# Output projection with the branch gate folded into w_out, a one-operation residual, and a separate pool for the head tiles

## The chip, the cores and the metric

The kernel runs as one program on one core of a Trainium2 chip. The metric is device time in microseconds (us) of one execution. All tensors are float32; large products are made of three float32r matmuls of a high and a low part (hi*hi, hi*lo, lo*hi).

## The reference, cut to what matters

One trunk layer over 2048 latent tokens of width 1024, with 256 context tokens as a prefix:

```
sh1, sc1, g1, sh2, sc2, g2 = split(silu(c) @ ada_w + ada_b, 6)
y = concat([rg_out, hg_out]) @ w_out        # RG-LRU heads and HGRN2 heads, both directions
h = layer_norm(ALPHA * h + g1 * y, ln1_g, ln1_b)
u2 = h * (1 + sc2) + sh2
f = hier_moe(u2)                            # top group, top 2 of its 8 experts, SwiGLU
h = layer_norm(ALPHA * h + g2 * f, ln2_g, ln2_b)
```

The gate g1 is a row of 1024 numbers, one for each output column of w_out.

## The kernel before

The kernel has four stages. A start of some 50 us makes the modulation of x. The **projection** (`project`, lines 773 to 870) runs to about 1049 us: 156 slots, each one projection of one 128-column unit of `w_in` over one block of tokens, in three passes over the tokens. After each slot the string `TURNS` says in which order evacuation, a step of the HGRN2 scan (`Head.run`), a step of the RG-LRU (`Lru`) and a filler step are issued. The **output stage** (lines 888 to 1212), here called stage F, takes the 16 tiles of 128 tokens through the output projection, the first layer norm and the router. Then come the expert blocks and the second layer norm.

What matters here in the projection: `mods` (line 362) is a generator that computes the rest of the modulation rows on GpSimd (POOL). Each of its 8 groups of 512 columns makes 8 loads of `ada_w` into the tile `mraw`, a multiplication (L371 or L373) and an addition (L374) on POOL for each, and a store to the DRAM row `modD` (L382); that is 17 steps a group, one or two steps a slot where no other filler waits. Groups 0 and 1 are g1. In the last pass the head scans store their backward states `kb` to `sbD` from POOL's queue (L556), and the RG-LRU stores its result `hb` to `rgD` the same way (L645). In the last six slots `wo_fetch` (L761) loads the 8 row blocks of `w_out` on SyncE (SP), and `wo_split` divides each into `woh` (a copy on ScalarE, ACT, L244) and `wol` (a subtraction, L245, on VectorE, DVE, but block 1 on POOL: `SPOOL = (1,)`). Block j = 7 is loaded into the buffer that block 1 had, so its load waits for block 1's split. The pools `hgp` (the heads' tiles), `tmp` and `ca` are closed together after the projection (`big.close()`), and all tiles of stage F are then laid in their place.

In stage F the order on every engine is written out by the loop of line 1155. In turn j it issues, among others: `post` of the previous tile's second half, `stats1`, the first `outproj` half of tile j (24 matmuls of 512 columns, with 8 transposes of a finished tile among them), `norm1`, part of the router's `top2`, `affine`, the rest of `top2` (L1079, L1081, L1083), `post` of tile j's first half, the multiplication L963 and the split L966/L972 (`mh` on ACT, `ml` on DVE) of the next tile's input, the second `outproj` half with the router's matmuls, and `place`. For the 10 tiles below token 1280 `head_norm` adds 4 small matmuls and `head_sum` a DVE addition (L942). `post` is:

```
dve.tensor_mul(r[:, s], d["ps"], g1[:, s])                                  # L991: PSUM times SBUF
dve.scalar_tensor_tensor(r[:, s], d["x"][:, s], ALPHA, r[:, s], ...)        # L992: SBUF and SBUF
dve.bn_stats(d["bs"][:, nh, :], r[:, s])                                    # L993
```

`affine` makes u2 on DVE (L1009, L1010) and at the same time scales the residual row on POOL (L1011, L1012, two operations over 128x1024 in SBUF). `constants` (L902) loads five rows broadcast to 128 partitions, 512 KB each (g1, l1g, l1b, l2g, l2b), and the router's weights; `loads` (L914) fetches a tile's inputs three turns ahead, all on SP.

Of the kernel before, what the change touches and what calls it, by code (L numbers as in the profile page):

```python
# [19 lines left out]
D = 1024  # L20
# [18 lines left out]
LE = L + 128  # L39
NRAW, NUP, NDOWN = 8, 9, 4  # L40
NWR, NUR = 2, 4
SPOOL = (1,)
EXTRA = (-9, -8, -2, -1)
MODS = (4, 8, 4)

# [29 lines left out]
def hymba_kernel(ctx, tc, xT, ctxT, x, small, rows, ada_w, w_in, gate_w, w_out, router_w, w1, w3, w2, out):  # L75
# [2 lines left out]

    dram = ctx.enter_context(tc.tile_pool(name="dram", bufs=1, space=DRAM))
    modD = dram.tile([1, 4096], F32, name="modD")  # L80
    oD = dram.tile([L, 512], F32, name="oD")
    hgD = dram.tile([512, L], F32, name="hgD")
    rgD = dram.tile([512, L], F32, name="rgD")
# [11 lines left out]
    big = ctx.enter_context(ExitStack())  # L95
    upool = early.enter_context(tc.tile_pool(name="upool", bufs=1))
    fk = early.enter_context(tc.tile_pool(name="fk", bufs=1))
    hgp = big.enter_context(tc.tile_pool(name="hgp", bufs=1))
    tmp = big.enter_context(tc.tile_pool(name="tmp", bufs=2))
    ca = big.enter_context(tc.tile_pool(name="ca", bufs=1))  # L100
    ident = const.tile([128, 128], F32, name="ident")
    make_identity(nc, ident)
    sm = ca.tile([128, 108], F32, name="sm")
# [246 lines left out]
    def proj(w, u, n, between, mid=3):  # L350
# [38 lines left out]
    class Head:  # L389
# [46 lines left out]
        def run(self):  # L436
# [108 lines left out]
            if p == 2:  # L545
                cur = S[:, h, 0, :]
                for half in (1, 0):
                    kb = hgp.tile([128, 5, 128], F32, name="kb", tag=f"keep{1 - half}")
                    carry = tmp.tile([128, 128], F32, name="carry", tag="S00", bufs=1)
                    for c in range(4, -1, -1):  # L550
                        if c == 4:
                            dve.tensor_copy(kb[:, c, :], cur)
                        nxt = kb[:, c - 1, :] if c else carry
                        dve.scalar_tensor_tensor(nxt, kb[:, c, :], fbs[:, h, 5 * half + c:5 * half + c + 1], U1[half][:, c, :], op0=ALU.mult, op1=ALU.add)
                    cur = carry
                    pool.dma_start(sbD[h][:, 640 * half:640 * half + 640], kb.rearrange("p c v -> p (c v)"))  # L556
                    yield


# [194 lines left out]
    def wo_fetch(m):  # L754
        while len(wraw) < min(m, KC):
            j = len(wraw)
            if j in (4, 5):
                wraw.append(upool.tile([128, D], F32, name="wr", tag="wr", bufs=2))
            else:
                wraw.append(fk.tile([128, D], F32, name="wor", tag="FK"[j % 2], bufs=2))  # L760
            sp.dma_start(wraw[j], w_out[128 * j:128 * j + 128, :])  # L761

    def wo_split():
        for j in range(KC):
# [106 lines left out]

    project()
    start.close()
    big.close()

    def rows_to(pl, name, lo, n=D, src=None):
        t = pl.tile([128, n], F32, name=name)
# [8 lines left out]
        return r  # L886

    with ExitStack() as st:
        fc = st.enter_context(tc.tile_pool(name="fc", bufs=1))
        fp = st.enter_context(tc.tile_pool(name="fp", bufs=2))  # L890
        fs = st.enter_context(tc.tile_pool(name="fs", bufs=2))
        st.enter_context(tc.manual_schedule())
        fk4 = [fk.tile([128, 2 * W], F32, name=n, tag=t, bufs=2) for n, t in (("g1", "F"), ("l1g", "K"), ("l1b", "F"), ("l2g", "K"))]
        g1, l1g, l1b, l2g = (t[:, :D] for t in fk4)
        l2b = fc.tile([128, D], F32, name="l2b")
        sc2 = fp.tile([128, D], F32, name="fu")
        rw = fk4[3][:, D:D + 40 * KC].rearrange("p (k e) -> p k e", e=40)
        rb = fc.tile([128, 40], F32, name="rb")
        dve.memset(rb[:, 4:8], FAR)
        dve.memset(rw[:, :, 4:8], 0.0)  # L900

        def constants():  # L902
            for t, src, lo in ((g1, modD, 0), (l1g, rows, 4096), (l1b, rows, 4096 + D), (l2g, modD, 2 * D), (l2b, modD, D), (rb[:, 0:4], rows, 4096 + 4 * D), (rb[:, 8:40], rows, 4100 + 4 * D)):
                n = t.shape[-1]
                sp.dma_start(t, src[0:1, lo:lo + n].to_broadcast([128, n]))
            rk = router_w.rearrange("(k p) e -> p k e", p=128)
# [7 lines left out]
        def loads(i):  # L914
            r0 = 128 * i
            d = M[i] = {}
            d["o"] = fp.tile([128, 4, 128], F32, name="fo", bufs=3)
            sp.dma_start(d["o"].rearrange("p h v -> p (h v)"), oD[r0:r0 + 128, :])
            if i < SPILL // 128:
                d["qb"] = fp.tile([128, 4, 128], F32, name="fqb", bufs=3)  # L920
                sp.dma_start(d["qb"], qbD[:, :, r0:r0 + 128].rearrange("h p t -> p h t"))
                d["sb"] = fp.tile([128, 4, 128], F32, name="fsb", bufs=3)
                sp.dma_start(d["sb"], sbD[:, :, r0:r0 + 128].rearrange("h p v -> p h v"))
            d["hg"] = fp.tile([128, 4, 128], F32, name="fhg", bufs=3)
            sp.dma_start(d["hg"], hgD[:, r0:r0 + 128].rearrange("(h p) t -> p h t", p=128))
            d["m"] = fp.tile([128, KC, 128], F32, name="fm", bufs=3)
            sp.dma_start(d["m"][:, 0:4, :], rgD[:, r0:r0 + 128].rearrange("(h p) t -> p h t", p=128))
            d["x"] = fp.tile([128, D], F32, name="fx", bufs=4)
            sp.dma_start(d["x"], x[r0:r0 + 128, :])
# [58 lines left out]
        def post(i, nh):  # L988
            d = M[i]
            r, s = d["r"], slice(512 * nh, 512 * nh + 512)  # L990
            dve.tensor_mul(r[:, s], d["ps"], g1[:, s])  # L991
            dve.scalar_tensor_tensor(r[:, s], d["x"][:, s], ALPHA, r[:, s], op0=ALU.mult, op1=ALU.add)  # L992
            dve.bn_stats(d["bs"][:, nh, :], r[:, s])  # L993

        def stats1(i):
# [4 lines left out]

        def norm1(i):
            r, mv, rs = (M[i][k] for k in ("r", "mv", "rs"))
            dve.scalar_tensor_tensor(mv[:, 0:1], mv[:, 0:1], -1.0, rs, op0=ALU.mult, op1=ALU.mult)
            act.activation(r, r, AF.Identity, scale=rs, bias=mv[:, 0:1])

        def affine(i):
# [29 lines left out]
        def top2(i):  # L1036
# [30 lines left out]
            yield  # L1067
            dve.max_index(ei, em, el)

            dve.tensor_sub(c[:, 3:4], em[:, 1:2], em[:, 0:1])  # L1070
            act.activation(c[:, 4:5], c[:, 3:4], AF.Exp)
            dve.tensor_copy(ee, ei[:, 0:2])
            yield
# [6 lines left out]
            yield  # L1080
            dve.reciprocal(wt[:, 0:1], c[:, 5:6])  # L1081
            yield
            dve.tensor_mul(wt[:, 1:2], wt[:, 0:1], c[:, 4:5])  # L1083

        def count(i):
            ee, ho, both = E.pop(i)
# [624 lines left out]
```

## Time and profile before

| what | value |
|---|---|
| median of 3 runs | 2267.64 us (2263.36 to 2269.0) |
| the profiled execution, its own time | 2266.98 us |
| its span from first to last instruction | 2265.3 us |
| TensorE matmul (PE) busy | 2055.4 us, 91% of the span |
| VectorE (DVE) busy | 1756.6 us, 78% |
| ScalarE (ACT) busy | 1167.5 us, 52% |
| GpSimd (POOL) busy | 667.9 us, 29% |
| mean granted TensorE clock | 0.956 of full speed |

Shares are averages over stages with different limits. In a timeline a row gives the start in us, the duration in us, engine, line, operation, output <- input, shape, count, and in brackets the idle time of that engine before it with what ended it. "x2" is two instructions merged. A duration holds also the time in which an instruction that has been started waits for a port.

### The profile page before, as it was taken

How to read it: one execution, taken by the hardware profiler on the slowest of the kernel's cores; microseconds unless marked ns; L12 is line 12 of the kernel's file. 1: busy time of each engine (PE TensorE's matmuls, PEld its weight loads, DVE VectorE, ACT ScalarE, POOL GpSimd, SP SyncE). 2: the span in 40 equal slices, each digit the busy share in tenths (PEclk: the TensorE clock that was granted, in tenths of full speed). 3: DMA queues.
4: the chain of work that ended last, by engine and by line, in shares of the span. 5: the costliest groups of instructions: out<-in, count | busy, mean ns of one | idle time of the engine just before them, and what ended most of it. 6: DMA issues, size and time to landing. Idle time of an engine off the chain costs nothing.

```text
span 2265.3 us, 34490 instructions
## 1 busy us (share of the span) xinstructions
PE 2055.4 (91%) x12440; PEld 1812.5 (80%) x12440; DVE 1756.6 (78%) x2665; ACT 1167.5 (52%) x1863; POOL 667.9 (29%) x507
## 2 busy tenths in 40 slices
PE   7999999999999999996899986999999999999970
PEld 3888788999988989986777775888888888888850
DVE  6677776766776898897788885788887778787869
ACT  3456554644654554654333323556666556566633
POOL 5122233223233130001555552122222222222216
PEclk9999999999999999998999996999999999999985
DMA  8233243323324143228555316789999898999965
GB/s 265 105 103 116 80 137 115 109 81 119 117 97 136 57 161 142 70 105 289 181 163 168 131 56 250 220 291 291 302 312 303 287 300 294 292 300 314 330 223 238
DMA packets 176275, 433.16 MB, mean 191 GB/s; under 512 B 26837, under 2 KB 68821, under 8 KB 175590
## 3 DMA queue, kind: packets, MB, share of 16 engines
q1 hardware_dynamic: 151846, 378.36, 47.7%
q0 software_dynamic: 14448, 45.23, 8.2%
q10 hardware_dynamic: 9808, 7.34, 1.0%
q8 instruction: 99, 1.62, 0.3%
q14 instruction: 74, 0.61, 0.1%
HBM read 354.43 MB, written 76.43 MB: 190 GB/s over the span
## 4 chain that ended last, share of the span: by engine, by line
PE 54%; DVE 20%; DMA 10%; ACT 6%; issue 6%; POOL 2%; SPq 1%; POOLq 0%; DVEq 0%; ACTq 0%
PE pp L354 8%; PE pp L355 8%; PE pp L356 8%; PE ph L1434 5%; PE pa L472 4%; DMA X<-u2D,ix 3%; DVE wlo L1297 3%; PE pg L596 3%; PE ph L1435 2%; PE pye L1324 2%; DMA ix<-idxD 2%; PE pye L1325 2%; PE pye L1323 2%; DVE fr L992 2%; PE ph L1379 2%
## 5 line engine op out<-in xcount | busy, mean ns | idle before, releaser
L1297 DVE TENSOR_TENSOR wlo<-raw,whi 128x1024 fp32r<-128x1024 f32 x384 | 452.3, 1221 | 56.4 <-ACT whi L1296 52.9
L354 PE MATMUL pp<-uh,wh 128*128 128x384 f32 (+2 forms) x1248 | 444.9, 356 | 3.2 <-ACT wh L244 1.8
L355 PE MATMUL pp<-ul,wh 128*128 128x384 f32 (+2 forms) x1248 | 428.8, 344 | 5.3 <-DVE ul L245 4.9
L356 PE MATMUL pp<-uh,wl 128*128 128x384 f32 (+2 forms) x1248 | 427.2, 342 | 3.2 <-DVE wl L245 3.2
L1296 ACT CAST whi<-raw 128x1024 fp32r<-128x1024 f32 x384 | 382.4, 1050 | 39.3 <-PE pye L1324 23.0
L1434 PE MATMUL ph<-xw,whi 128*128 128x448 f32 (+3 forms) x896 | 257.6, 363 | 1.6 <-DVE hid L1385 1.6
L354 PEld LDWEIGHTS pp<-uh,wh 128*128 128x128 f32 x1248 | 238.1, 191 | 23.7 <-ACT rgs L597 5.2
L355 PEld LDWEIGHTS pp<-ul,wh 128*128 128x128 f32 x1248 | 238.1, 191 | 20.8 <-DVE ul L245 11.2
L356 PEld LDWEIGHTS pp<-uh,wl 128*128 128x128 f32 x1248 | 237.4, 190 | 13.2 <-DVE wl L245 4.3
L1435 PE MATMUL ph<-xw,wlo 128*128 128x224 f32 (+3 forms) x896 | 221.7, 247 | 0.0
L373 POOL TENSOR_SCALAR mraw<-mraw,sil 128x512 f32<-128x512 f32 x56 | 103.1, 1842 | 358.3 <-DMA mraw<-in_ada_w_dram 358.3
L1333 POOL DMA_INDIRECT accD<-y,ix x46 | 107.7, 2341 | 315.0 <-DVE y L1332 302.3
L1377 PE MATMUL ph<-whi,xx 128*80 128x256 f32 (+3 forms) x608 | 176.0, 290 | 4.7 <-DMA raw<-in_w_dram 3.6
L1434 PEld LDWEIGHTS ph<-xw,whi 128*128 128x128 f32 x896 | 173.3, 193 | 7.2 <-DVE hid L1385 1.8
L1435 PEld LDWEIGHTS ph<-xw,wlo 128*128 128x128 f32 x896 | 176.0, 196 | 1.2
L1379 PE MATMUL ph<-wlo,xx 128*80 128x256 f32 (+3 forms) x608 | 173.1, 285 | 1.9 <-DVE wlo L1297 1.9
L1378 PE MATMUL ph<-whi,xx 128*80 128x256 f32 (+3 forms) x608 | 172.0, 283 | 0.0
L1306 POOL DMA_INDIRECT X<-u2D,ix x46 | 70.1, 1525 | 322.2 <-DMA ix<-idxD 202.8
L472 PE MATMUL pa<-Q,km 128*128 128x128 f32 x896 | 125.5, 290 | 16.1 <-DVE Q L475 10.3
L472 PEld LDWEIGHTS pa<-Q,km 128*128 128x128 f32 x896 | 120.3, 196 | 21.3 <-ACT km L462 7.1
L245 DVE TENSOR_TENSOR wl<-wr,wh 128x1024 fp32r<-128x1024 f32 x84 | 107.9, 1285 | 37.2 <-ACT wh L244 37.1
L982 PE MATMUL py<-woh,mh 128*128 128x512 f32 x256 | 116.6, 455 | 16.3 <-ACT mh L966 16.3
(351 smaller groups left out, 4552.3 us busy)
## 6 DMA issues: line engine op xcount, KB each, us to landing
raw<-in_w_dram SPq DMA_DIRECT2D x384, 512.0 KB
wr<-in_w_in_dram SPq DMA_DIRECT2D x84, 512.0 KB
mraw<-in_ada_w_dram SPq DMA_DIRECT2D x64, 256.0 KB
aw<-in_ada_w_dram SPq DMA_DIRECT2D x16, 512.0 KB
fx<-in_x_dram SPq DMA_DIRECT2D x16, 512.0 KB
accD<-fr SPq DMA_DIRECT2D x16, 512.0 KB
u2D<-fu SPq DMA_DIRECT2D x16, 512.0 KB
f<-accD SPq DMA_DIRECT2D x16, 512.0 KB
```

The source lines that it names most:

```text
L354: pe.matmul(ps, wh[:, k, :], uh[:, k, :], start=k == 0, stop=False)
L355: pe.matmul(ps, wh[:, k, :], ul[:, k, :], start=False, stop=False)
L356: pe.matmul(ps, wl[:, k, :], uh[:, k, :], start=False, stop=k == KC - 1)
L472: pe.matmul(pa[:, c, :], km[:, s:s + 128], cut(Q, s, [(2 * b, 64 // b), (T + b, 2), (1, b)]), start=True, stop=True)
L982: pe.matmul(ps, mh[:, k, :], wo[k][0][:, s], start=k == 0, stop=False)
L1296: act.copy(hi, raw)
L1297: dve.tensor_sub(lo, raw, hi.bitcast(F32))
L1377: pe.matmul(p, self.xh[:, k, :], wh[:, kk, :], start=k + g == 0, stop=False, skip_group_check=True)
L1378: pe.matmul(p, self.xl[:, k, :], wh[:, kk, :], start=False, stop=False, skip_group_check=True)
L1379: pe.matmul(p, self.xh[:, k, :], wl[:, kk, :], start=False, stop=k == KC - 1, skip_group_check=True)
L1434: pe.matmul(p[:, :2 * n], wh[:, kk, f], self.x[:, k].rearrange("p h t -> p (h t)"), start=k == 0, stop=False)
L1435: pe.matmul(p[:, :n], wl[:, kk, f], self.x[:, k, 0, :], start=False, stop=k == KC - 1)
```

## The change

w_out is multiplied by the gate once, column by column, while the projection runs: a new generator `gated`, called by `mods` after groups 0 and 1, broadcasts 512 gate values to 128 partitions, and for each of 8 row blocks loads 128x512 of `w_out`, multiplies on POOL and stores to a DRAM tensor `woD` from POOL's queue. `wo_fetch` reads `woD`. `post` is then one operation on PSUM and x, and the load of g1 in `constants` goes. The heads' pool `hgp` lies on the other side of the memory and is closed first; a pool `fl` with the loaded inputs of stage F takes its place. All splits of w_out are on DVE, the `sbD` stores go from POOL's queue to SP's, two memsets from DVE to POOL, and four tiny operations of two tensors become operations of a tensor and a per-partition scalar.

```diff
-SPOOL = (1,)
+SPOOL = ()
...
+    woD = dram.tile([D, D], F32, name="woD")
...
-    hgp = big.enter_context(tc.tile_pool(name="hgp", bufs=1))
     tmp = big.enter_context(tc.tile_pool(name="tmp", bufs=2))
     ca = big.enter_context(tc.tile_pool(name="ca", bufs=1))
+    heads = ctx.enter_context(ExitStack())
+    hgp = heads.enter_context(tc.tile_pool(name="hgp", bufs=1, side="right"))
...
+    def gated(nh):
+        s = slice(512 * nh, 512 * nh + 512)
+        g = tmp.tile([128, 512], F32, name="g1h", tag="macc", bufs=1)
+        sp.dma_start(g, modD[0:1, s].to_broadcast([128, 512]))
+        for k in range(KC):
+            raw = tmp.tile([128, 512], F32, name="wog", tag="mraw", bufs=1)
+            sp.dma_start(raw, w_out[128 * k:128 * k + 128, s])
+            yield
+            pool.tensor_mul(raw, raw, g)
+            pool.dma_start(woD[128 * k:128 * k + 128, s], raw)
+            yield
...
             sp.dma_start(modD[:, 512 * g:512 * g + 512], r)
+            if g < 2:
+                yield from gated(g)
...
-                    pool.dma_start(sbD[h][:, 640 * half:640 * half + 640], kb.rearrange("p c v -> p (c v)"))
+                    sp.dma_start(sbD[h][:, 640 * half:640 * half + 640], kb.rearrange("p c v -> p (c v)"))
...
-            sp.dma_start(wraw[j], w_out[128 * j:128 * j + 128, :])
+            sp.dma_start(wraw[j], woD[128 * j:128 * j + 128, :])
...
     project()
     start.close()
-    big.close()
+    heads.close()
...
+        fl = st.enter_context(tc.tile_pool(name="fl", bufs=3, side="right"))
+        big.close()
...
-        dve.memset(rb[:, 4:8], FAR)
-        dve.memset(rw[:, :, 4:8], 0.0)
 
         def constants():
-            for t, src, lo in ((g1, modD, 0), (l1g, rows, 4096), ...
+            pool.memset(rb[:, 4:8], FAR)
+            pool.memset(rw[:, :, 4:8], 0.0)
+            for t, src, lo in ((l1g, rows, 4096), ...
...
-            d["o"] = fp.tile([128, 4, 128], F32, name="fo", bufs=3)
+            d["o"] = fl.tile([128, 4, 128], F32, name="fo", bufs=3)
...
-            dve.tensor_mul(r[:, s], d["ps"], g1[:, s])
-            dve.scalar_tensor_tensor(r[:, s], d["x"][:, s], ALPHA, r[:, s], op0=ALU.mult, op1=ALU.add)
+            dve.scalar_tensor_tensor(r[:, s], d["x"][:, s], ALPHA, d["ps"], op0=ALU.mult, op1=ALU.add)
...
-            dve.scalar_tensor_tensor(mv[:, 0:1], mv[:, 0:1], -1.0, rs, op0=ALU.mult, op1=ALU.mult)
+            dve.tensor_scalar(mv[:, 0:1], mv[:, 0:1], rs, -1.0, op0=ALU.mult, op1=ALU.mult)
...
-            dve.tensor_sub(c[:, 3:4], em[:, 1:2], em[:, 0:1])
+            dve.tensor_scalar(c[:, 3:4], em[:, 1:2], em[:, 0:1], None, op0=ALU.subtract)
...
-            dve.tensor_mul(wt[:, 1:2], wt[:, 0:1], c[:, 4:5])
+            dve.tensor_scalar(wt[:, 1:2], wt[:, 0:1], c[:, 4:5], None, op0=ALU.mult)
```

## Rows read from the trace of the kernel before

**Rows 1.** Windows view, stage F: busy PE, PEld, DVE, ACT, POOL; clock, DMA.

```profile
1200.00:1250.00 50.00, 45.36 (x242) 38.17 (x241) 44.58 (x107) 19.24 (x57) 25.94 (x27) 0.97 0.56 174
```

**Rows 2.** Starts of post for tiles 3 and 16, from the chain of waits.

```profile
1107.90 0.70 DVE fr L991
...
1343.29 0.69 DVE fr L991
```

**Rows 3.** Timeline of TensorE from one tile's first matmul to the next.

```profile
1222.98 0.48 PE L982 MATMUL py<-woh,mh 128*128 128x512 f32 x1
1224.07 0.50 PE L983 MATMUL py<-woh,ml 128*128 128x512 f32 x1 [0.61 <-DVE ml L972]
...
1230.36 1.05 PE L936 MATMUL pob<-fsb,fqb 128*128 128x128 f32 x8
...
1240.82 0.49 PE L982 MATMUL py<-woh,mh 128*128 128x512 f32 x1 [1.23 <-ACT mh L966]
```

**Rows 4.** Timeline of VectorE in one turn of stage F.

```profile
1215.00 0.21 DVE L1079 TENSOR_SCALAR c<-c 128x1 f32<-128x1 f32 x1
...
1215.45 1.90 DVE L1083 TENSOR_TENSOR tok<-tok,c 128x1 f32<-128x1 f32 x1
1217.27 0.68 DVE L991 TENSOR_TENSOR fr<-py,g 128x512 f32<-128x512 f32 x1
1217.98 2.38 DVE L992 SCALAR_TENSOR_TENSOR fr<-fx,fr 128x512 f32<-128x512 f32 x1
```

**Rows 5.** Timeline of GpSimd in the same turn.

```profile
1213.91 3.43 POOL L1011 TENSOR_TENSOR fr<-fr,l1g 128x1024 f32<-128x1024 f32 x1 [2.83 <-DVE fu L1009]
1217.41 2.40 POOL L1012 TENSOR_TENSOR fr<-fr,l1b 128x1024 f32<-128x1024 f32 x1
```

**Rows 6.** All instructions of three lines: count, then shortest/median/longest in ns.

```profile
L992 DVE SCALAR_TENSOR_TENSOR fr<-fx,fr x32: 691/1139/2383, 1080.9 to 1348.6; 128x512 f32<-128x512 f32 x32
...
L1083 DVE TENSOR_TENSOR tok<-tok,c x16: 160/1900/1917, 1124.7 to 1372.2; 128x1 f32<-128x1 f32 x16
...
L1079 DVE TENSOR_SCALAR c<-c x16: 205/206/208, 1124.2 to 1371.7; 128x1 f32<-128x1 f32 x16
```

**Rows 7.** A wide tensor-with-scalar operation of the projection, all 48 of its line.

```profile
L404 DVE TENSOR_SCALAR F<-F,omlb,lbc x48: 399/476/1470, 53.1 to 953.2; 128x384 f32<-128x384 f32 x32, 128x256 f32<-128x256 f32 x8, 128x512 f32<-128x512 f32 x8
```

**Rows 8.** Timeline of VectorE from the projection's end into stage F.

```profile
1051.27 0.06 DVE L899 MEMSET rb<- 128x4 f32 x1 [1.68 <-DMA sbD<-kb]
...
1052.79 4.51 DVE L245 TENSOR_TENSOR wol<-wor,woh 128x1024 fp32r<-128x1024 f32 x2
...
1062.49 0.09 DVE L900 MEMSET l2g<- 128x32 f32 x1
...
1075.13 0.69 DVE L1181 TENSOR_SCALAR fu<-l2g 128x1024 f32<-128x1024 f32 x1 [3.69 <-DMA l2g<-modD]
```

**Rows 9.** Timelines of GpSimd, SyncE's queue and TensorE over the same stretch.

```profile
1065.13 0.20 POOL L884 TENSOR_SCALAR rstd<-ms 128x4 f32<-128x4 f32 x1 [8.91 <-ACT g L950]
...
1045.68 10.89 SPq L761 DMA_DIRECT2D wor<-in_w_out_dram  x2
...
1070.22 0.79 PE L982 MATMUL py<-woh,mh 128*128 128x512 f32 x1 [1.91 <-ACT mh L966]
```

**Rows 10.** Timeline of VectorE behind the last tile.

```profile
1358.68 2.24 DVE L1097 TENSOR_TENSOR ho<-ho,pos 128x64 f32<-128x64 f32 x1
```

**Rows 11.** Additions and stores of mods; SyncE's longest waits: total, times, longest us.

```profile
L374 POOL TENSOR_TENSOR macc<-macc,mraw x56: 1262/1294/2275, 83.3 to 841.9; 128x512 f32<-128x512 f32 x56
...
L382 SPq DMA_DIRECT2D modD<-mr x8: 231/242/251, 166.9 to 859.2; - x8
...
SPq L234 <- DVE wl L245: 508.3, 71, 20.1
SPq L368 <- POOL macc L374: 82.7, 18, 8.5
```

**Rows 12.** The eight stores of sbD from GpSimd's queue (tile view): time to landing.

```profile
DMA to landing us min/median/max: 7.7/7.8/7.9
```

More of the change, by code (lines that the diff above doesn't have):

```diff
@@ L892, in hymba_kernel @@
         st.enter_context(tc.manual_schedule())
-        fk4 = [fk.tile([128, 2 * W], F32, name=n, tag=t, bufs=2) for n, t in (("g1", "F"), ("l1g", "K"), ("l1b", "F"), ("l2g", "K"))]
-        g1, l1g, l1b, l2g = (t[:, :D] for t in fk4)
+        fk4 = [fk.tile([128, 2 * W], F32, name=n, tag=t, bufs=2) for n, t in (("sq", "F"), ("l1g", "K"), ("l1b", "F"), ("l2g", "K"))]
+        l1g, l1b, l2g = (t[:, :D] for t in fk4[1:])
         l2b = fc.tile([128, D], F32, name="l2b")
@@ L898, in hymba_kernel @@
         rb = fc.tile([128, 40], F32, name="rb")
-        dve.memset(rb[:, 4:8], FAR)
-        dve.memset(rw[:, :, 4:8], 0.0)
         def constants():
-            for t, src, lo in ((g1, modD, 0), (l1g, rows, 4096), (l1b, rows, 4096 + D), (l2g, modD, 2 * D), (l2b, modD, D), (rb[:, 0:4], rows, 4096 + 4 * D), (rb[:, 8:40], rows, 4100 + 4 * D)):
+            pool.memset(rb[:, 4:8], FAR)
+            pool.memset(rw[:, :, 4:8], 0.0)
+            for t, src, lo in ((l1g, rows, 4096), (l1b, rows, 4096 + D), (l2g, modD, 2 * D), (l2b, modD, D), (rb[:, 0:4], rows, 4096 + 4 * D), (rb[:, 8:40], rows, 4100 + 4 * D)):
                 n = t.shape[-1]
@@ L916, in loads @@
             d = M[i] = {}
-            d["o"] = fp.tile([128, 4, 128], F32, name="fo", bufs=3)
+            d["o"] = fl.tile([128, 4, 128], F32, name="fo", bufs=3)
             sp.dma_start(d["o"].rearrange("p h v -> p (h v)"), oD[r0:r0 + 128, :])
             if i < SPILL // 128:
-                d["qb"] = fp.tile([128, 4, 128], F32, name="fqb", bufs=3)
+                d["qb"] = fl.tile([128, 4, 128], F32, name="fqb", bufs=3)
                 sp.dma_start(d["qb"], qbD[:, :, r0:r0 + 128].rearrange("h p t -> p h t"))
-                d["sb"] = fp.tile([128, 4, 128], F32, name="fsb", bufs=3)
+                d["sb"] = fl.tile([128, 4, 128], F32, name="fsb", bufs=3)
                 sp.dma_start(d["sb"], sbD[:, :, r0:r0 + 128].rearrange("h p v -> p h v"))
-            d["hg"] = fp.tile([128, 4, 128], F32, name="fhg", bufs=3)
+            d["hg"] = fl.tile([128, 4, 128], F32, name="fhg", bufs=3)
             sp.dma_start(d["hg"], hgD[:, r0:r0 + 128].rearrange("(h p) t -> p h t", p=128))
-            d["m"] = fp.tile([128, KC, 128], F32, name="fm", bufs=3)
+            d["m"] = fl.tile([128, KC, 128], F32, name="fm", bufs=3)
             sp.dma_start(d["m"][:, 0:4, :], rgD[:, r0:r0 + 128].rearrange("(h p) t -> p h t", p=128))
```

## The prediction

> **What bounds the kernel now.** I read the page first: TensorE is busy most of the span, VectorE next. The slices of the page show TensorE near full in the projection and below it in stage F, so I took the windows of that stage: of 50 us TensorE is busy 45.4 and VectorE 44.6, at a clock of 0.97 [rows 1]. Neither is full, so each waits for the other somewhere. The chain of waits tells which leads: through stage F it runs along VectorE's `post`, `affine` and the split of the next tile, turn after turn. From tile 3 to tile 16 `post` starts at 1107.90 and at 1343.29 [rows 2]: 13 turns of 18.1 us. In the turn that I copied, TensorE's first matmul is 17.84 us from the next tile's first, and it waits twice, 0.61 us for `ml` and 1.23 us for `mh`, both made behind `post` [rows 3]. Without the waits its turn is 17.84 - 0.61 - 1.23 = 16.0 us. So VectorE sets the turn, and TensorE's own work is the next bound, 2.1 us below.
>
> **What VectorE loses time on.** Two operations of that turn are long without having much to do: L1083 multiplies one element per partition in 1.90 us, and L992 takes 2.38 us for 512 [rows 4]. The same lines take 0.16 and 0.69 us at their shortest [rows 6]. The reason is in GpSimd's timeline. L1011 ends at 1217.34, and L1083 ends at 1217.35; L1012 ends at 1219.81, and L992 0.55 us behind it, about its own working time [rows 4, 5]. An operation of VectorE that reads two tensors from SBUF stands until the operation on GpSimd is over. L991, which reads PSUM and one tensor from SBUF, started at 1217.27, had L1012 beside it for most of its time, and took 0.68 [rows 4, 5]. L1079, a tensor with a scalar, ran inside L1011 in 0.21 [rows 4, 5], and none of its 16 took more than 0.208 [rows 6].
>
> **The change, part by part.**
>
> *`post` and the tiny operations.* L991 goes from both halves: 2 x 0.68 = 1.36 us a turn. The new L992 reads x from SBUF and the product from PSUM, as L991 did, so I take 0.69 us and no standing: 2.38 - 0.69 = 1.69 less. Its bounds are 0.69 and 2.38; L991 is the nearest row. L1083 becomes the form of L1079: 1.90 - 0.16 = 1.74 less, bounds 0 and 1.74. The other two changed forms (L1003, L1070) I cost at nothing: they stood beside no GpSimd operation, and the forms are alike in length. VectorE's turn falls by 4.8 us, from 18.1 to 13.3, which is below TensorE's 16.0. So TensorE becomes the bound and only 2.1 of the 4.8 us is gained: what is late next is the projection's matmuls themselves. Ten of the 13 turns contain `head_norm`, whose eight rows span 1.05 us and overlap their neighbours [rows 3]; I take 0.9 off for the other three. After: 10 x 16.0 + 3 x 15.1 = 205.3 us against 235.4. **Gain 30.1 us**; if every turn needs 16.0, 27.4. The split L972 (two SBUF tensors) may now meet the end of L1012, since it comes earlier; it needs its result only 16 us after the tile began, and VectorE has 2.7 us to spare.
>
> A rule of the Trainium skill speaks against the L1083 part. The row first: a wide operation of a tensor with scalars in SBUF, L404, has a median of 0.48 us and a longest of 1.47 [rows 7]; that form can stand too. The Trainium skill (VectorE: DVE Perf Modes, The perf-mode tier table) gives `tensor_scalar` on float32 in SBUF the doubled mode, which by SBUF — State Buffer (SBUF: two separate sides) needs the port pair shared with GpSimd. By that rule the new L1083 stands like the old one and VectorE's turn is 13.3 + 1.74 = 15.0 us instead of 13.3; still under 16.0, so the sum stays, with 1.0 us to spare instead of 2.7. The one-element rows of L1079 say that it doesn't stand [rows 6].
>
> *The start of stage F.* Before, a memset of VectorE stands 1.68 us for a store of `sbD` in the middle of the last RG-LRU piece, and two splits take 4.51 us instead of 2 x 1.22, beside GpSimd's split of block 1 [rows 8]; SP stands at the load of block 7 for most of 10.89 us, because that split is late, and stage F's loads are behind it [rows 9]. After: 1.68 + 2.07 less, one split of 1.22 more on VectorE, so the last split ends 2.5 us earlier than 1062.5. More is possible, since the loads of the first tiles may start while the RG-LRU still holds its pool. But the memset of `rw` is now in GpSimd's queue and waits for block 7's split, about 1060.0; behind it stands the first tile's `rstd`, which ran at 1065.13 [rows 9], so at most 5.1. I take 3.5. One of the three 512 KB rows ahead of l2g in SP's order goes; VectorE waited 3.69 us for l2g [rows 8], of which I take a third, 1.3 (bounds 0 and 3.69). The first two tiles have no router work beside them; the first halves of their `post` lose 0.68 each: 1.4. **Gain 6.2 us**, bounds 3.9 (2.5 + 0 + 1.4) and 10.2 (5.1 + 3.7 + 1.4).
>
> *The end of stage F.* Behind the last tile L991's 0.68 goes. L1083's 1.74 does not come back: L1097 reads two SBUF tensors and stands for the same L1012 until 1360.9 [rows 10]. **Gain 0.7**, at most 2.4.
>
> *The detour of w_out in the projection.* `gated` adds 32 steps to the 136 of `mods`. I counted through the slots: with one or two steps a slot there are 171 places, so the last store moves from slot 125 to slot 151 of 156, and none is left for the end. Issued work: 18 loads on SP, 16 multiplications and 16 stores on GpSimd, 8 MB of traffic in a stage that leaves most of its DMA time idle. GpSimd is under a third busy and has nothing else that anyone waits for. An addition of this size takes 1.29 us there [rows 11], and a VectorE operation can stand that long: 16 x 1.29 = 20.6 us at worst, if each one hit and TensorE had no slack; and the `mods` work that ended at 859 us [rows 11] now runs beside the last pass. Nothing excludes a small gain in the early slots, which are lighter. I take **2 us lost**, bounds 0 and 8, near the low end because TensorE, not VectorE, sets most slots. The `sbD` stores wait for VectorE on SP instead of on GpSimd; behind them stand weight loads that are two units ahead, so nothing.
>
> **The sum.** 30.1 + 6.2 + 0.7 - 2.0 = 35.0 us. The profiled execution took 2266.98, 0.66 below the median of the runs; 2266.98 - 35.0 = 2232.
>
> **The rivals.**
>
> *VectorE stays the bound.* If the new `post` still stands for GpSimd, the 1.69 us of L992 stay; if L1083 stands too, only 1.36 us a turn goes: 13 x 1.36 = 17.7 instead of 30.1, so 2244. For it: the operation that is kept, L992, is the one that stood [rows 4]. Against: it read two SBUF tensors then, and L991, which has the new kind of inputs, did not stand. Chance 0.13.
>
> *SP becomes the bound of the early projection: slower.* The tile `mraw` is single, so each load of `gated` waits on SP until the store before it has landed. Nearest row: GpSimd's `sbD` stores land 7.8 us after issue [rows 12]; with 1.29 for the multiplication SP could stand 9 us, 16 times, 145 us, and the weight loads stand behind it. Above 2.2 us a step that reaches TensorE, the 35 us are lost and the kernel is slower; at 4 us it is 2232 + 64 = 2296. For it: SP already stood 82.7 us at these loads. Against: at the weight loads SP stands 508.3 us for VectorE, 71 times [rows 11], so it comes to them early by 7 us on average. Chance 0.04.
>
> *It comes out even.* The standing in the last pass eats the gain: 29 us or more, above the bound of 20.6 from multiplications alone, so it would need the moved `mods` work as well; 2260 to 2274. Chance 0.05.
>
> **How the numbers follow.** The forecast has 0.78. Its own range runs from 2224 (10.2 at the start, 2.4 at the end, nothing lost in the projection) to 2243 (27.4, 3.9 and 0.7 gained, 8 lost). The range takes in the first rival's 2244 and its spread: 2221 to 2247. A measurement tells 0.3%, 7 us, from no change. Faster: 0.78 + 0.13 = 0.91; same 0.05; slower 0.04.
>
> **What would show it.** Right: `post` starts 16.0 us apart, new L992 at 0.69 in both halves, L1083 near 0.2, TensorE without waits in the turn and its clock at 1.00 there, first matmul of stage F at 1065 to 1068, the last `modD` store near 1020. Wrong: L992 above 1 us, VectorE without idle time in stage F, waits of SP at the `woD` steps followed by waits of TensorE on `wl`, or a projection that ends after 1055.

## The result and the profile after

The changed kernel takes 2238.47 us in the median of 4 runs (2232.19 to 2243.1), beside 2265.5 for the kernel before: ratio 0.9872, 95% interval 0.9852 to 0.9893. The forecast was 2232, range 2221 to 2247. The profiled execution took 2243.1 us, its span is 2241.0 instead of 2265.3. It is the slowest of its four, so the spans differ by 24.3 us where the medians differ by 27.0. The two spans, cut at the same events:

| stretch | before | after | difference | forecast |
|---|---|---|---|---|
| start to the last L354 (now L356) matmul of the projection | 1048.39 | 1065.66 | +17.3 | +2.0 |
| to stage F's first matmul | 21.8 | 17.3 | -4.5 | -3.5 |
| to `post` of tile 3 | 37.7 | 35.0 | -2.7 | -2.7 |
| 13 turns of stage F | 235.4 | 199.3 | -36.1 | -30.1 |
| `post` of tile 16 to the first expert matmul (L1377, now L1395) | 36.4 | 36.5 | +0.2 | -0.7 |
| the rest | 885.6 | 887.2 | +1.5 | 0 |

So stage F gave more than forecast and the projection took back far more. The windows view of stage F (columns as in [rows 1]):

```profile
1150.00:1200.00 50.00, 50.00 (x285) 43.16 (x284) 40.26 (x111) 21.38 (x66) 33.67 (x30) 1.00 0.58 181
```

TensorE is busy for all of the 50 us; [rows 1] had 45.36. The first halves of `post` for tiles 3 and 16, from VectorE's timeline, answer to [rows 2]:

```profile
1118.01 0.68 DVE L1010 SCALAR_TENSOR_TENSOR fr<-fx,py 128x512 f32<-128x512 f32 x1
...
1317.31 0.68 DVE L1010 SCALAR_TENSOR_TENSOR fr<-fx,py 128x512 f32<-128x512 f32 x1
```

That is 13 turns of 15.33 us instead of 18.1. One turn of VectorE, to be read beside [rows 4]:

```profile
1192.31 1.22 DVE L1028 TENSOR_TENSOR fu<-fu,l2b 128x1024 f32<-128x1024 f32 x1
...
1193.89 0.21 DVE L1101 TENSOR_SCALAR tok<-tok,c 128x1 f32<-128x1 f32 x1
1194.02 0.68 DVE L1010 SCALAR_TENSOR_TENSOR fr<-fx,py 128x512 f32<-128x512 f32 x1
...
1197.13 2.23 DVE L991 TENSOR_TENSOR ml<-fm,mh 128x1024 fp32r<-128x1024 f32 x1 [0.52 <-ACT mh L985]
...
1201.54 0.69 DVE L1010 SCALAR_TENSOR_TENSOR fr<-fx,py 128x512 f32<-128x512 f32 x1 [1.26 <-PE py L1003]
```

GpSimd in the same turn, as in [rows 5]:

```profile
1192.36 3.44 POOL L1029 TENSOR_TENSOR fr<-fr,l1g 128x1024 f32<-128x1024 f32 x1 [3.83 <-DVE fu L1027]
1195.88 2.41 POOL L1030 TENSOR_TENSOR fr<-fr,l1b 128x1024 f32<-128x1024 f32 x1
```

Both L1101 and the `post` behind it run inside L1029 without standing; the split L991 is what now stands, until L1030 ends at 1198.29. And VectorE has come to wait for TensorE (1.26 us in the last row). All instructions of the three lines (shortest, median, longest ns), for [rows 6]:

```profile
L1010 DVE SCALAR_TENSOR_TENSOR fr<-fx,py x32: 673/684/689, 1092.3 to 1323.5; 128x512 f32<-128x512 f32 x32
...
L1101 DVE TENSOR_SCALAR tok<-tok,c x16: 213/214/215, 1133.1 to 1346.4; 128x1 f32<-128x1 f32 x16
...
L991 DVE TENSOR_TENSOR ml<-fm,mh x16: 1225/2233/2828, 1083.0 to 1305.8; 128x1024 fp32r<-128x1024 f32 x16
```

**Where the projection loses.** I took, for each slot, the start of its first matmul and subtracted that of before. Up to slot 128 the difference goes to and fro between -2.0 and +1.4 us (both within slots 20 to 63, in which all of `gated` runs; behind them, at slot 64, it is 0.4). It is -0.6 at slot 132, 5.1 at slot 133, 7.3 at 139, 12.2 at 145, 17.3 at 152. There the last pass folds the RG-LRU back, and there the rest of `mods` now stands: the last `modD` store moved from 859.2 us [rows 11] to 1050.0. The windows view of that stretch, slot 132 to the end, first of before (two of its rows and their sum), then of after:

```profile
891.00:911.00 20.00, 18.56 (x103) 16.71 (x102) 18.75 (x26) 7.78 (x13) 1.08 (x2) 1.00 0.31 114
...
971.00:991.00 20.00, 18.47 (x109) 16.61 (x108) 18.95 (x27) 7.13 (x14) 1.08 (x2) 1.00 0.32 118
...
sum 157.00, PE 151.64 PEld 145.10 DVE 136.30 ACT 83.20 POOL 5.94; mean PE 18.95 PEld 18.14 DVE 17.04 ACT 10.40 POOL 0.74
```

```profile
890.00:910.00 20.00, 15.41 (x78) 14.83 (x77) 17.92 (x21) 4.53 (x8) 9.61 (x8) 0.83 0.52 184
...
970.00:990.00 20.00, 15.01 (x83) 14.69 (x82) 18.06 (x25) 3.73 (x7) 9.25 (x8) 0.91 0.67 235
...
sum 175.00, PE 159.89 PEld 151.13 DVE 151.20 ACT 83.43 POOL 45.12; mean PE 17.77 PEld 16.79 DVE 16.80 ACT 9.27 POOL 5.01
```

GpSimd has 45.1 us of work instead of 5.9, VectorE needs 151.2 us instead of 136.3 for its part, and TensorE's clock is at 0.83 and 0.91 in the two rows shown, where it was 1.00. By the two sums TensorE's work takes 8.3 us longer (159.9 for 151.6) and its idle time grows by 9.8 (15.1 for 5.4). TensorE's waits in the stretch (total, times, longest us), before and after:

```profile
PE pa L454 <- DVE k L446: 2.9, 2, 1.5
```

```profile
PE pa L471 <- DVE k L463: 9.6, 2, 5.0
```

The first of the two waits, in the timelines of VectorE, TensorE and GpSimd of after:

```profile
890.93 1.82 DVE L657 TENSOR_TENSOR_SCAN hb<-fw,hst 128x768 f32<-128x768 f32 x1 [1.20 <-DMA rgD<-hb]
...
892.97 1.65 DVE L660 TENSOR_TENSOR hb<-hb,rr 128x768 f32<-128x768 f32 x1
...
895.53 0.95 DVE L463 TENSOR_TENSOR k<-K 128x768 f32<-128x768 f32 x1
...
896.54 2.93 PE L471 MATMUL pa<-q,k 128*128 128x128 f32 x12 [4.59 <-DVE k L463]
...
899.59 0.52 PE L357 MATMUL pp<-ul,wh 128*128 128x384 f32 x1
...
884.49 1.43 POOL L389 TENSOR_TENSOR macc<-macc,mraw 128x512 f32<-128x512 f32 x1
885.87 0.60 POOL L662 DMA_DIRECT2D rgD<-hb  x1
889.79 1.56 POOL L388 TENSOR_SCALAR mraw<-mraw,sil 128x512 f32<-128x512 f32 x1 [3.32 <-DMA mraw<-in_ada_w_dram]
891.44 2.37 POOL L389 TENSOR_TENSOR macc<-macc,mraw 128x512 f32<-128x512 f32 x1
```

The store of `rgD` stands behind an addition of `mods`, so the next scan waits 1.20 us for the single `hb`; L660 (0.96 us without company) stands beside L389. `k` comes 2.6 us later than before (895.53 against 892.92), TensorE idles 4.59 us and then works at the lower of its two levels, 1.2 GHz: the windows view grants it 0.50 behind the wait, and a matmul of 384 columns takes 0.52 us, as against 0.34 in the same place before:

```profile
896.50:899.50 3.00, 2.96 (x13) 2.96 (x14) 2.21 (x2) 0.00 (x0) 0.46 (x2) 0.50 0.40 158
```

```profile
892.92 0.95 DVE L446 TENSOR_TENSOR k<-K 128x768 f32<-128x768 f32 x1
...
893.93 1.60 PE L454 MATMUL pa<-q,k 128*128 128x128 f32 x12 [1.42 <-DVE k L446]
...
895.55 0.34 PE L355 MATMUL pp<-ul,wh 128*128 128x384 f32 x1
```

In figures: 4.59 - 1.42 = 3.2 us more idle, 2.93 - 1.60 = 1.3 in L471, and 9 projection matmuls that start within 2.91 us (899.12 to 902.03) instead of 1.56 (9 x 0.173, their spacing before), 1.4. Together 5.9; slot 133 shows 5.7.

Two things could make `k` late: VectorE's own operations last longer because they stand beside GpSimd's, or VectorE waits for the single `hb`, whose store is late in GpSimd's queue. VectorE's waits for `rgD` from slot 132 on, before and after, are the same in size, so it is mainly the first:

```profile
DVE hb L640 <- DMA rgD<-hb: 2.1, 1, 2.1
```

```profile
DVE hb L657 <- DMA rgD<-hb: 1.6, 2, 1.2
```

I compared every operation of VectorE in that stretch with the median of its line and shape in the whole execution. In after 14 are more than 0.15 us longer, by 9.9 us together; 9 of them began inside an addition L389 (8.1 us) and 5 inside a multiplication L386 or L388 (1.8). Before has none.

### The profile page after: what moved, and what is told of

Same layout as the page of the kernel before. It is cut to its first block, busy times and chain, and to the rows that moved or that the text cites. A ratio compares the mean times of both kernels' runs of the same rounds, so it can differ in the third digit from the quotient of the medians.

```text
span 2241.0 us, 34527 instructions
## 1 busy us (share of the span) xinstructions
PE 2048.3 (91%) x12440; PEld 1810.6 (81%) x12440; DVE 1713.6 (76%) x2632; ACT 1167.9 (52%) x1863; POOL 700.3 (31%) x532
## 5 line engine op out<-in xcount | busy, mean ns | idle before, releaser
L356 PE MATMUL pp<-uh,wh 128*128 128x384 f32 (+2 forms) x1248 | 445.5, 357 | 4.6 <-ACT uh L246 2.3
L356 PEld LDWEIGHTS pp<-uh,wh 128*128 128x128 f32 x1248 | 238.5, 191 | 26.3 <-ACT rgs L614 5.9
L388 POOL TENSOR_SCALAR mraw<-mraw,sil 128x512 f32<-128x512 f32 x56 | 99.7, 1780 | 363.1 <-DMA mraw<-in_ada_w_dram 363.1
L1351 POOL DMA_INDIRECT accD<-y,ix x46 | 113.1, 2459 | 316.5 <-DVE y L1350 315.9
L1395 PE MATMUL ph<-whi,xx 128*80 128x256 f32 (+3 forms) x608 | 175.3, 288 | 3.7 <-ACT whi L1314 3.5
L1324 POOL DMA_INDIRECT X<-u2D,ix x46 | 65.5, 1425 | 320.8 <-PE pye L1343 134.3
L489 PE MATMUL pa<-Q,km 128*128 128x128 f32 x896 | 124.0, 288 | 19.2 <-DVE Q L492 11.9
L490 DVE COPY_PREDICATED A<-masks,pa 128x384 f32<-128x384 uint8 (+1 forms) x140 | 84.1, 618 | 46.9 <-PE pa L489 44.1
```

Source lines behind the costliest of these rows:

```text
L356: pe.matmul(ps, wh[:, k, :], uh[:, k, :], start=k == 0, stop=False)
L489: pe.matmul(pa[:, c, :], km[:, s:s + 128], cut(Q, s, [(2 * b, 64 // b), (T + b, 2), (1, b)]), start=True, stop=True)
L1351: pool.indirect_dma_start(out=accD, out_offset=bass.IndirectOffsetOnAxis(ap=ix[:n, 0:1], axis=0), in_=y[:n], in_offset=None, compute_op=AL ...
L1395: pe.matmul(p, self.xh[:, k, :], wh[:, kk, :], start=k + g == 0, stop=False, skip_group_check=True)
```

## The experiments

Theory A: the projection's loss is the `mods` work of GpSimd, moved beside a stretch in which VectorE is close to the bound. All kernels read alike: the difference to before of a slot's first matmul at slot 128, at the last slot, 155, and what was lost between.

| kernel | median us | ratio to before, 95% | slot 128 | slot 155 | between |
|---|---|---|---|---|---|
| after | 2238.47 | 0.9872 (0.9852 to 0.9893) | -0.6 | 17.3 | 17.8 |
| x1_early | 2243.56 | 0.9906 (0.9878 to 0.9934) | 17.7 | 20.5 | 2.7 |
| x2_late | 2284.3 | 1.0076 (1.0053 to 1.0099) | 1.4 | 17.9 | 16.5 |
| x3_tiny | 2239.36 | 0.9893 (0.9851 to 0.9935) | -0.3 | 15.5 | 15.7 |
| x4_post2 | 2247.03 | 0.9903 (0.9873 to 0.9933) | 6.5 | 23.3 | 16.8 |
| x5_rgd_act | 2242.1 | 0.9917 (0.9886 to 0.9947) | 5.2 | 24.3 | 19.2 |
| x6_sbd_pool | 2242.08 | 0.9889 (0.9856 to 0.9923) | 3.7 | 20.4 | 16.6 |
| x8_mid | 2258.03 | 0.9963 (0.9939 to 0.9987) | 33.4 | 33.5 | 0.1 |
| x10_nomul | 2556.03, once | not comparable | 0.6 | 4.7 | 4.1 |
| y1_323 | 2232.65 | 0.9845 (0.9819 to 0.987) | 5.4 | 9.7 | 4.3 |
| y2_422 | 2234.03 | 0.9867 (0.9841 to 0.9893) | 7.7 | 13.9 | 6.2 |
| y4_act | 2256.55 | 0.9964 (0.9946 to 0.9982) | 16.9 | 36.0 | 19.1 |
| y5_fin | 2228.63 | 0.9831 (0.9806 to 0.9856) | 2.9 | 7.1 | 4.2 |

x3, x4 and x6 run the projection up to slot 128 with the same `mods` as after and still differ there by 0.3 to 7.1 us: so much goes from one execution to another, and the slots of each row are those of one execution. The last column is steadier: 15.7 to 17.8 in after, x3, x4 and x6.

**x2_late: the kernel before, with `mods` late and nothing else.**

```diff
             sp.dma_start(modD[:, 512 * g:512 * g + 512], r)
+            if g < 2:
+                for _ in range(2 * KC):
+                    yield
```

> Kernel before, with 16 empty steps in mods behind each of its first two groups: no gated, no woD, everything else as before, but the last modD store moves from slot 125 to slot 151. Theory A: this alone costs what the projection lost in the change: last unit's first matmul at 1060 to 1066 instead of 1048.4, time 2265 + 12 to 17 = 2277 to 2282 us. Rival B (sbD on SP, the heads' pool or the third VectorE split): no change, 2263 to 2268.

It loses 16.5 us in the same slots, and 18.3 in all (2266.0 beside it), the whole of after's loss and 2 us more than the range expected. Its waits view names the same wait:

```profile
PE pa L457 <- DVE k L449: 9.3, 2, 5.2
```

So neither `gated`, the `sbD` stores, the pools nor the third split is needed for the loss; the late steps alone make it.

**x10_nomul: after, without most of the multiplications and additions of the last three groups.**

```diff
-                else:
+                elif g < 5:
                     pool.tensor_scalar(raw, raw, sil[:, k, 0:1], None, op0=ALU.mult)
```

> Kernel after, without the multiplications and additions of GpSimd (L388, L389) for k of 1 to 7 in the last three groups of mods; their loads stay. So these groups' sums hold only one of eight terms, and what comes behind the projection is computed from other numbers; only the projection is read. Theory A: the loss from slot 132 on goes to within 3 us of nothing, last unit at 1047 to 1052. If the loads on SP and their traffic were the cause, nothing changes: 1062 to 1067.

4.1 us instead of 17.8 are lost behind slot 128, with all loads in place; that is a little more than the 3 us expected, and the last unit comes at 1053.1 instead of 1047 to 1052. Its 2556.03 us say nothing, since what follows the projection computes from other numbers. The waits and the windows from slot 132 on:

```profile
PE pa L471 <- DVE k L463: 3.6, 2, 2.0
```

```profile
891.39:1053.08 161.69, 154.76 (x959) 146.06 (x959) 140.34 (x225) 83.47 (x134) 6.25 (x8) 1.00 0.42 144
```

```profile
890.22:1065.66 175.44, 160.33 (x959) 151.57 (x958) 151.82 (x225) 83.43 (x134) 44.90 (x32) 0.96 0.40 136
```

Both rows run from slot 132's first matmul to the last one, the first of x10, the second of after. VectorE does this stretch in 140.3 us instead of 151.8, so 11.5 us of its time go with GpSimd's work, most of them the 9.9 us of lengthened operations above; the clock is back at 1.00, and the loss is 13.7 smaller.

**x5_rgd_act: after, with the `rgD` stores on ScalarE's queue.**

```diff
-                pool.dma_start(rgD[128 * t:...], hb)
+                act.dma_start(rgD[128 * t:...], hb)
```

> Kernel after, with the rgD stores issued from ScalarE's queue instead of GpSimd's, so that they no longer stand behind the mods multiplications; those stay where they are, late. Theory Q (the loss comes from the order of GpSimd's queue: store late, next scan waits for the single hb): the waits of VectorE for DMA rgD<-hb fall below 1 us in total after slot 130, and most of the 17.3 us comes back: last unit at 1050 to 1056, time 2223 to 2230. Theory P (the loss comes from VectorE's operations standing for the mods operations themselves): waits for rgD go, but the long hb, scan and wl operations stay; last unit at 1060 to 1066, time 2233 to 2240. Rival: ScalarE now waits for hb and its evacuations come late; time above 2240.

The waits for `rgD` are gone from VectorE's list, the loss is not: 19.2 us. TensorE's wait in it:

```profile
PE pa L471 <- DVE k L463: 11.0, 2, 5.8
```

The standing is still there: L481 takes 1251 ns in the mean of this stretch, 1083 in after and 955 (L464) before. So taking the stores out of GpSimd's order does not help in this tail, which speaks for theory P. But 2242.1 us lies in the range of the third rival: ScalarE now waits for `hb`, 20.4 us in two places before L435 alone, and VectorE waits 4.4 us for `q` from it. So this run alone doesn't show that the queue costs nothing there; after's own 1.6 us of waits for `rgD` show that it costs little.

**x1_early: the steps of `mods` denser in all passes.** `MODS = (4, 8, 4)` becomes `(2, 2, 2)`.

> Kernel after, with two steps of mods in every second slot instead of every fourth or eighth, so that the last modD store falls in slot 123 of 156 (125 before the change, 151 after it). Theory A: the 17.3 us that the projection lost come from the mods work of GpSimd beside the last pass's tail. Then the last unit's first matmul comes at 1048 to 1052 (1065.7 after the change) and the time is 2238 - 15 = 2223 us, 2220 to 2227; PE waits at L471 for k fall from 9.6 us to about 3. Rival B: the loss comes from the sbD stores on SP, from the other place of the heads' tiles in SBUF, or from the third split on VectorE, none of which depends on when mods runs. Then the last unit stays at 1064 to 1067 and the time at 2236 to 2241. Rival C: early in the projection the denser steps cost as much as the late ones did: the loss moves to slots 5 to 100 and the time stays within 3 us of 2238.

The loss behind slot 128 goes (2.7), as theory A has it, but 17.7 us are lost before it: 5.5 from slot 40 to 43, 6.4 at slot 121. That is rival C in kind, but 6.4 us of the loss lie behind the slots 5 to 100 that it named, and the time is 5 us above 2238, not within 3. The loss at slot 121 in VectorE's and GpSimd's timelines:

```profile
825.28 1.82 DVE L657 TENSOR_TENSOR_SCAN hb<-fw,hst 128x768 f32<-128x768 f32 x1 [6.93 <-DMA rgD<-hb]
...
816.58 1.73 POOL L388 TENSOR_SCALAR mraw<-mraw,sil 128x512 f32<-128x512 f32 x1 [13.61 <-DMA mraw<-in_ada_w_dram]
818.39 1.29 POOL L389 TENSOR_TENSOR macc<-macc,mraw 128x512 f32<-128x512 f32 x1
819.63 0.61 POOL L662 DMA_DIRECT2D rgD<-hb  x1
```

Here the queue does cost: GpSimd waits 13.61 us for a load of `mraw`, an `hb` that was finished at 811.3 stands behind it, and VectorE waits 6.93 us for its store.

**x8_mid: denser in the second pass alone.** `MODS = (4, 1, 4)`.

> Kernel after, with two steps of mods in every slot of the second pass (every eighth before) and the spacing of the other passes kept. The last modD store then falls in slot 114 of 156, and no mods work stands beside the fold-back of the RG-LRU pieces from slot 120 on. The denser steps of x1_early cost 10 us up to slot 43 and 7 us at slot 120 and only 1.6 us between slots 44 and 112. Theory A, refined (mods work hurts where VectorE is close to the bound or where GpSimd's queue holds rgD stores behind it, and is free elsewhere): last unit's first matmul at 1048 to 1053, time 2238 - 13 to 17 = 2221 to 2227 us. Rival: two steps in every slot of the second pass wait for the single mraw buffer and hold SP's weight loads: slots 44 to 99 lose 10 us or more and the time stays at 2235 to 2245.

Nothing is lost behind slot 128, but 36 us in the second pass. The rival has the place, but 2258.03 us is more than its 2245, and the path is another: SP stands 63.7 us at the `mraw` loads between 470 and 640 us, yet TensorE waits for no weights. It is held at the matmul that closes a group and needs GpSimd's last addition, its only wait between 470 and 680 us:

```profile
PE pmr L395 <- POOL macc L389: 27.5, 3, 12.1
```

**x6_sbd_pool: after, with `sbD` on GpSimd's queue again.** In L573 `sp` becomes `pool`.

> Kernel after, with the sbD stores back on GpSimd's queue. If the stores on SP cost nothing, as the prediction has it, and those on GpSimd cost nothing either, the time stays within 4 us of 2238 and the last unit at 1063 to 1068. If the place on GpSimd is worse now that late mods work stands there, kb is freed later and the projection gets longer by 2 to 8 us. If SP was part of the loss, the last unit comes 3 us or more earlier.

No difference that shows (16.6 lost behind slot 128, the last unit at 1068.7, the time 3.6 us from after's): neither queue of these stores costs anything that one can see here.

**x3_tiny and x4_post2: each half of the change in stage F alone.** x3 undoes L1021, L1088 and L1101; x4 undoes `post`:

```diff
-            dve.scalar_tensor_tensor(r[:, s], d["x"][:, s], ALPHA, d["ps"], op0=ALU.mult, op1=ALU.add)
+            dve.tensor_copy(r[:, s], d["ps"])
+            dve.scalar_tensor_tensor(r[:, s], d["x"][:, s], ALPHA, r[:, s], op0=ALU.mult, op1=ALU.add)
```

> Kernel after, with the three one-element operations (L1021, L1088, L1101) in their old forms, the one-operation post kept. L1101 reads two SBUF tensors again and should stand for L1029 on GpSimd, 1.5 to 2 us. If TensorE is the bound with more than 1.7 us of VectorE time to spare, post stays 15.3 to 15.6 us apart and the time within 3 us of 2238; L991, which stands about 1 us now, may stand less. If VectorE has less to spare than that, the turn grows to 16.5 to 17 us and the time to 2253 to 2259.

> Kernel after, with post in two operations again: a copy of the product from PSUM into r, then the old residual of two SBUF tensors; the one-element operations keep their new forms. The prediction priced the half of the change that lies in post at 1.36 + 1.69 = 3.05 us of VectorE a turn, and the other half at 1.74. By that, VectorE's turn is 13.3 + 3.05 = 16.3, just over TensorE's 15.5: post 16.3 us apart, time 2238 + 13 x 0.8 = 2248 to 2252 (VectorE bound by 0.8 us). If the one-element operation was the larger part, nothing moves: 2236 to 2242. If post was all of it, the turn goes back to 18 us: 2238 + 33 = 2271.

In x3 the turn is 15.51 us (tile 3's `post` at 1115.9, tile 16's at 1317.51), in x4 15.69 (1128.14 to 1332.15); by the prices x4 should have had 16.3. In x3 L1101 stands again and L991 no longer does:

```profile
L1101 DVE TENSOR_TENSOR tok<-tok,c x16: 159/1898/1912, 1131.0 to 1344.8; 128x1 f32<-128x1 f32 x16
...
L991 DVE TENSOR_TENSOR ml<-fm,mh x16: 1224/1226/2822, 1081.6 to 1305.7; 128x1024 fp32r<-128x1024 f32 x16
```

In x4 the residual of two SBUF tensors is back. The median of its 32 mixes two kinds: the second halves run free at 0.69, the first halves stand for GpSimd again, but 13 of the 16 by 0.9 us (1.59) and not by the 1.69 of the price. They now begin 1.0 us before the end of GpSimd's first operation, where L992 had begun early in the second:

```profile
L1011 DVE SCALAR_TENSOR_TENSOR fr<-fx,fr x32: 691/704/2185, 1101.0 to 1337.9; 128x512 f32<-128x512 f32 x32
...
1161.41 1.59 DVE L1011 SCALAR_TENSOR_TENSOR fr<-fx,fr 128x512 f32<-128x512 f32 x1
...
1159.02 3.42 POOL L1030 TENSOR_TENSOR fr<-fr,l1g 128x1024 f32<-128x1024 f32 x1 [2.87 <-DVE fu L1028]
```

So either half gives most of the gain (33.8 and 31.4 of 36.1 us), since TensorE is the bound behind both (busy 50.00 and 49.24 us of 50 from 1150 to 1200); prices of single stands do not add.

**y4_act: the multiplications of `mods` on ScalarE.** L388 becomes `act.activation(raw, raw, AF.Copy, scale=...)`.

> Kernel after, with the multiplication of mods (L388, 1.6 us each on GpSimd) on ScalarE for k of 1 to 7; the additions (L389) and the order stay. About 57 of 100 parts of GpSimd's mods time go. Theory A with the standing as its cause: L388 reads one tensor and a scalar, L389 two tensors; the loss from slot 132 on falls to about half, 8 us, time 2228 to 2232. If only the additions make VectorE stand, the loss stays at 14 to 17 us: 2236 to 2241. Rival: ScalarE waits for the mraw loads in its order, and its evacuations come late: above 2243.

The rival: ScalarE stands for the loads, 100.2 us in 27 places, and the loss grows to 36.0.

```profile
ACT mraw L388 <- DMA mraw<-in_ada_w_dram: 100.2, 27, 9.5
```

This run therefore cannot tell what of the standing is due to L388 and what to L389. After's own trace tells it for that execution: 8.1 of the 9.9 us fell on operations that began inside an addition, 0.4 to 1.1 us each, and 1.8 on operations that began inside a multiplication, 0.2 to 0.4 each.

**y1_323, y2_422, y5_fin: a spacing that avoids both.** y1 has `MODS = (3, 2, 3)`, y2 `(4, 2, 2)`.

> Kernel after, with two steps of mods in every third slot of passes 0 and 2 and every second of pass 1; last modD store in slot 130, before the fold-back tail. Two steps in every slot of the second pass jammed (x8_mid lost 14, 12 and 9 us at three groups) and two in every second slot of it cost 2.4 us in 70 slots (x1_early). Theory A: nothing lost from slot 132 on, 3 to 8 us before it, so last unit at 1052 to 1057 and the time 2226 to 2232 us. Rival: earlier groups meet the pieces of the transitions (slots 40 to 43, 121) as in x1_early and lose 12 us or more there: 2235 to 2243.

> As y1_323, with pass 0 at every fourth slot as in the kernel after, and passes 1 and 2 at every second; last modD store in slot 130. The dense steps of the third pass are those with which x1_early lost 6.4 us at slot 121, where VectorE waited 6.93 us for an rgD store behind mods work. Theory A: no loss in slots 0 to 43, some 2 in pass 1, 0 to 7 at slot 121, none after 132: 2225 to 2233 us. Rival: as for y1_323, 2235 to 2243.

Both lose less behind slot 128, 4.3 and 6.2 us, and all of that by slot 133, where the last group of `mods` ends; from there to slot 155 nothing more is lost, as theory A has it. y1 loses 5.4 before slot 128 and comes out at 2232.65, y2 7.7 and 2234.03, each about 1 us above what was expected. In y1 TensorE's list has the wait of x8_mid again; y5 is y1 with that closing matmul one step later (the core of its edit, with a comment of mine):

```diff
+                if k == 0 and late is not None:
+                    yield
+                    yield from late     # mr load, one step, L395, addition, modD store of group g - 1
```

> y1_323 with the end of each group of mods from the third on (its matmul L395, the addition and the modD store) one step later, between the first load and the first multiplication of the next group; the number of steps stays. In y1_323 TensorE waited 8.2 us in three places for macc at that matmul, because two steps in a slot bring it too soon behind the addition on GpSimd. If these waits are what is left of the loss, they fall below 3 us, the last unit comes at 1050 to 1054 and the time is 2226 to 2229 us. Rival: the next group's first load is then held longer by the single macc, the groups slip and the waits come back elsewhere: 2231 to 2236.

The wait in y1, then in y5 (where the line is L384):

```profile
PE pmr L395 <- POOL macc L389: 8.2, 3, 3.6
```

```profile
PE pmr L384 <- POOL macc L403: 3.1, 1, 3.1
```

y5_fin takes 2228.63 us, the fastest of all: ratio 0.9831 to before, where after has 0.9872; the two intervals just meet. Its last L356 matmul comes at 1055.47, a little later than expected, and the wait is at 3.1 where below 3 was expected; 10 us of the 17.3 are back. The 4.2 us that it still loses behind slot 128 fall at slots 131 and 132, where its one wait of 3.1 us stands (at 893.0).

## Why the prediction was right, and where it was wrong

The sum came out 6 us low, by two errors that partly cancel. That the range held is luck: with the projection's 17.3 us and the other terms as forecast the sum would have been 2266.98 - 30.1 - 6.2 - 0.7 + 17.3 = 2247.3, above it.

- **The detour of w_out failed.** "I take 2 us lost, bounds 0 and 8": the projection lost 17.3. What I priced, the 16 multiplications (1.31 us each on GpSimd, in light slots), cost nothing that shows. What I named in half a sentence and gave no price, the `mods` work that "now runs beside the last pass", was nearly all of it: x2_late loses 16.5 of the 17.8 us by the place of this work alone. Behind slot 132 it is 12 additions and 13 multiplications. I also put the value near the low end "because TensorE, not VectorE, sets most slots"; in slots 132 to 150 it is VectorE that TensorE waits for, and then TensorE's clock falls: beside 9.8 us more idle time its work takes 8.3 us longer. The windows of before show that stretch: VectorE busy 18.75 and 18.95 of 20 us where TensorE has 18.5. I had not read them. Bounded like the others, 13 multiplications of 1.57 us (median of L373) and 12 additions of 1.29 [rows 11] that VectorE can stand for give up to 36 us; a bound of 8 was too small by its own method.
- **The turns of stage F were right in mechanism, mis-sized in the bound.** TensorE took over, as said. Its turn is 15.5 us and not 16.0: I subtracted the idle time from one matmul's end to the next one's start, but matmuls overlap, so a wait costs more. In the turn that I copied L983 starts 1.09 us behind L982 and the next tile's L982 1.54 us behind L1034; in after these steps take 0.32 and 0.14. So the two waits cost 2.2 us and not 1.84. Ten turns of 15.5 and three shorter ones are 199.3; gain 36.1 for 30.1.
- **The new `post` and L1101** took 0.68 and 0.21 us, as their nearest rows had it. The rule of the Trainium skill (VectorE: DVE Perf Modes, The perf-mode tier table; SBUF — State Buffer (SBUF: two separate sides)) by which L1101 would stand is not borne out for one element: 0.213 to 0.215 us in all 16, 14 of them inside L1029. The row of that table is for 2048 elements. The split L991, foreseen as the one that may stand, does, by 1.0 us, and TensorE waits nowhere in the turns. That an operation of two SBUF tensors stands until GpSimd's is over holds where GpSimd's began first; L1028 below is the other case.
- **Start and end of stage F**: 4.5 + 2.7 for 6.2; the 0.7 at the end does not show up to the first expert matmul (36.5 us for 36.4). Which part of the start's gain belongs to the pools and which to the splits was not tried apart.
- **SyncE at `gated`**: the rival's wait exists, 38.7 us in 7 places at the loads of `wog`, the longest 9.9, near the 9 us of its price. It reached no slot, because SP's waits for `wl`, 165.3 us in that stretch before, fell to 153.0: SP came early, as argued against it.
- **The signs to look for**: "a projection that ends after 1055" was listed as wrong, and it was. By the signs for right, stage F's first matmul was to come at 1065 to 1068 and the last `modD` store near 1020; they came at 1083.0 and 1050.0. The `post`, L1083's new form and the clock of 1.00 in stage F came as listed.

The rows behind TensorE's turn, to be read beside [rows 3], one of before and four of after:

```profile
1239.28 0.31 PE L1034 MATMUL pl<-l2g,uT 128*128 128x40 f32 x2
```

```profile
1193.68 0.47 PE L1001 MATMUL py<-woh,mh 128*128 128x512 f32 x1
1194.00 0.39 PE L1002 MATMUL py<-woh,ml 128*128 128x512 f32 x1
...
1199.50 0.31 PE L1052 MATMUL pl<-l2g,uT 128*128 128x40 f32 x2
1199.64 0.48 PE L1001 MATMUL py<-woh,mh 128*128 128x512 f32 x1
```

The 1.5 us of the rest I cannot place; no line behind stage F was changed but in number, and executions of the same work differ by more (up to 7 us by slot 128).

## What to carry to other kernels

When a change adds steps to a background generator, the price is not at the added steps but where the generator's last steps come to lie: read the windows of that stretch for the engine that is nearest to full. Background work has a place where it is cheapest, between a tail that has no slack and a density at which its own buffers and queues jam; both ends were dear here (17.8 us in after's tail, 17.7 in x1_early ahead of it) and the middle, y5_fin, cost 7. Where the next bound lies close, price a change by that bound alone, measured where that engine is full, and don't add up what single operations lose.

## What the runs showed of the hardware that was not expected

- A scan of two SBUF tensors stands for GpSimd as other two-tensor operations do: L657 takes 1.80 to 1.82 us alone and 2.89 where it began 0.01 us behind an addition L389. A tensor-tensor operation with a per-partition scalar (L571, 128x128) goes from a mean of 0.352 to 0.449 us.
- Additions of two tensors on GpSimd hold VectorE, multiplications by a per-partition scalar far less: of the 9.9 us that VectorE's operations lost in after behind slot 132, 8.1 fell on operations that began inside an addition and 1.8 on those that began inside a multiplication. The scan at 890.93 began 1.1 us into L388, which lasted 1.56, and took its usual 1.82; the four operations that L388 held were released about 0.5 us after its start, not at its end (spans on GpSimd are rough).
- Who begins first holds. L1028 (two SBUF tensors) begins 0.05 us ahead of GpSimd's L1029 in all 16 tiles and takes its 1.22 to 1.23 us; L1029 then takes 3.39 to 3.47, L1030 of the same shape 2.34 to 2.43. There GpSimd stands.
- Standing shifts. With L1101 standing 1.7 us (x3_tiny) L991 runs free, with L1101 free L991 stands 1.0: an operation that was held arrives later at the next one, behind GpSimd's end.
- The clock makes a wait of TensorE dearer than it is long: 3.2 us more idle became 5.9, with a granted clock of 0.50 behind the wait.
